# Six blocks instead of three between a gate matrix and its weights, one-hots one step earlier, low parts off GpSimd, and another order at the end of an encoder layer

## The chip, the cores and the metric

The kernel runs on one core of one Trainium2 chip. The metric is the device time of one execution in microseconds (us); the version before is the median of three runs. The core's engines are TensorE (PE in the rows: matmuls; PEld: its weight loads), VectorE (DVE), ScalarE (ACT), GpSimd (POOL) and SyncE (SP, which here only issues DMAs). Each engine works through its own instructions in order.

## The reference

One encoder layer for 512 tokens of width 2048, all in float32:

```
h = RMSNorm(x);  [q | k | v | x_gate | x_rec] = h @ W_in
A = windowed attention(q, k, v)              # 16 heads, 128-query blocks, a sink per head
B = gelu(x_gate) * (RG-LRU forward + RG-LRU backward)(conv(x_rec))
x = x + concat(RMSNorm(A), RMSNorm(B)) @ W_out
x = x + PEER(RMSNorm(x))                     # below
return RMSNorm(x)

PEER: q = xt @ W_pq -> 8 heads x 2 halves; top 16 of 128 keys in each half, top 16 of the sums:
      128 experts (of 16384) for each token, with softmax gates
      act = gelu(x . u_emb[e]);  out = sum over e of gate * act * v_emb[e]
```

## The kernel before

**Matmuls in three parts.** Every float32 operand is split into a high part `hi` (a cast on ScalarE, line 269) and a low part `lo = raw - hi` (a subtraction, line 281), and a product is three matmuls: hi by hi, hi by lo, lo by hi (`mm3`, lines 296 to 299). The weights come in units of 128 by 2048 (1 MB): `load` issues the DMA on SP into one of two `raw` buffers, `split` casts `hi` into one of two buffers and lists the low part, `flush_lo` makes the listed low parts, `take` splits up to the unit after the one that it hands out. So a unit's hi cast can start when the unit two before it has been multiplied. In the first stages `split` makes the low part at once; from the projection W_pq on (`st["defer"]`) it is made where `flush_lo` is called. `on_pool` (line 241) names nine units whose low part is made on GpSimd: seven that belong to W_out, split during the attention, and the first two of W_pq.

**Attention** (lines 704 to 834) is a generator with three steps for each of 32 pairs of heads and query blocks: scores (TensorE `ps_s`, VectorE mask, maximum and the small additions of lines 719 to 721), exponentials (ScalarE) with the transposes of an earlier pair, and the product with V (`ps_o`, VectorE `y_att`, line 757). Two more steps after each eight pairs transpose the output (`att_yt`). One step follows each of the 16 `mm3` of a W_out unit, so that the attention runs beside W_out's matmuls. `ps_s` and `ps_o` share two PSUM banks.

**The experts, in two ways.** 160 of the tokens (128 and `NB1` = 32) are done by gathering rows of u_emb and v_emb with indirect DMAs on GpSimd and multiplying on VectorE; `gather_gen` does one such step (some 2.3 us of VectorE) whenever it is called, a "tick". The other 352 tokens (`TD`) are done densely: 128 U blocks compute act for all experts (`u_block`: 16 times `mm3`, 48 matmuls, then a gelu into `ga`), and 16 groups of 8 V units multiply the weighted activations by v_emb (`v_unit`, also 48 matmuls each). In between, `weigh` multiplies `ga` by the gate matrix `G` (VectorE, line 1321) and splits the result into `Wh` (ScalarE, line 1324) and `Wl` (VectorE, line 1325). U blocks run ahead of their weighing; an activation that must wait long is spilled to DRAM (`ad`) and read back (`reload`, on SP, into three buffers `gr`).

**The gate matrix** is built in 88 steps of `NB` = 4 tokens beside the U blocks. `g_onehots` compares two lists of indices with an iota (one-hots `ohA` and `ohB`, two VectorE operations) and scales `ohA` by the gates, with one VectorE multiplication for even steps and four ScalarE operations for odd ones. `g_step` n first copies the result of step n-2 out of PSUM (`flush_evac`, ScalarE, line 1219, four banks `psA`), makes the one-hots of step n+3 (`G_AHEAD`), and multiplies ohB by ohA into `ps_G`. After each eight steps ScalarE issues a 2 MB DMA into `gd` in DRAM. `load_g` reads G back for four blocks at a time, on SP, once `gd` is written.

**The order** is fixed by `stage_plan` before anything runs: it keeps a clock for TensorE, VectorE and ScalarE, and puts tasks (routing, softmax, gate steps, ticks) into hooks, four per U block, each with costs in us. The first `lead0` = 40 U blocks come before any V unit: 37 with hooks, and three more, beside which the first nine blocks are weighed:

```
    load_g(0)
    load_g(1)
    for _ in range(3):
        reload()
    for i in range(3):
        u_block(lead0 - 3 + i, beside=lambda: beside(range((0, 3, 6)[i], (3, 6, PR + LEAD)[i])))
```

Then 8 V units and a run of U blocks alternate: six runs of three U blocks, one of seven, and eight or seven from there. `beside` makes, in this order, a tick if one is due, the low part, the additions of the V unit before (`v_evict`), the weighings, and further ticks. 55 activations are spilled.

**The end.** The last group has no U blocks. `final(q)` transposes a quarter of the accumulated output for three groups of tokens (twelve transposes into PSUM tiles `pt_f` of two pools with two banks each), adds the residual (VectorE, line 1451), and `out_piece` squares it on ScalarE into a tile `jk` of one of these pools and multiplies it by the final gain on GpSimd. Quarters 0 to 2 follow V units 5, 6 and 7; quarter 3 follows the last `v_evict`.

Of the kernel before, what the change touches and what calls it, by code (L numbers as in the profile page):

```python
# [8 lines left out]
F32 = mybir.dt.float32  # L9
# [32 lines left out]
LEAD = 1  # L42
NB = 4
G_AHEAD = 3
G_STEPS = [(tt, t) for tt in range(1, NT) for t in range(NB1 if tt == 1 else 0, 128, NB)]

C_GMIX = 0
# [10 lines left out]
def stage_plan():  # L58

    tasks = []
    for r in range(6):
        tasks += [("pair", 6.9, 0.0, 0.0)]
        if r < 4:
            tasks += [("tr", 0.0, 0.6, 0.6), ("sc", 6.8, 0.6, 1.3)]  # L70
        if r < 5:
            tasks += [("pick", 0.0, 2.5, 0.0)]
        tasks += {2: [("soft_a", 0, 0.9), ("soft_b", 0, 1.5), ("prime", 0.0, 0.0, 0.0)],
                  3: [("soft_a", 1, 0.9), ("soft_b", 1, 1.5)],
                  4: [("rep", 0.8, 0.0, 0.7)],
                  5: [("soft_a", 2, 1.7), ("free", 0.0, 0.0, 0.0), ("lists", 1), ("soft_b", 2, 1.7),
                      ("lists", 2)]}.get(r, [])
    tasks += [("pre", m) for m in range(G_AHEAD)]
    for n in range(len(G_STEPS)):
        if G_STEPS[min(n + G_AHEAD + 2, len(G_STEPS) - 1)] == (3, 0):  # L80
            tasks += [("lists", 3)]
        tasks += [("g", n)]
    hooks, ticks_on, since = [], False, 0.0
    pe, dve, act = 0.0, 4.0, 0.0
    while tasks:
        if len(hooks) % 4 == 0:
            dve, act = dve + 2.35, act + 2.4
        pe += 1.94
        cur = []
        while tasks and max(dve, act) <= pe:  # L90
            if ticks_on and since >= 3.5:
                cur.append(("tick", None))
                dve, since = dve + 2.35, 0.0
                continue
            t = tasks.pop(0)
            if t[0] == "g":
                cost, arg = ((1.37, 2.2, 1.22), (2.06, 0.6, 1.22))[t[1] % 2], t[1]
            elif t[0] == "pre":
                cost, arg = ((2.06, 0.0, 0.0), (1.37, 1.6, 0.0))[t[1] % 2], t[1]
            elif t[0] == "lists":  # L100
                cost, arg = (0.0, 0.5, 0.9), t[1]
            elif t[0] in ("soft_a", "soft_b"):
                cost, arg = (t[2], 0.5, 0.0), t[1]
            else:
                cost, arg = t[1:], None
            cur.append((t[0], arg))
            dve, act, pe = dve + cost[0], act + cost[1], pe + cost[2]
            if t[0] == "prime":
                ticks_on, since = True, -9.0
            if ticks_on:  # L110
                since += cost[0]
            if t[0] in ("tr", "soft_a", "lists"):
                break
        dve, act = max(dve, pe - 2), max(act, pe - 2)
        hooks.append(cur)
    nbg = -(-len(hooks) // 4)
    hooks += [[] for _ in range(4 * nbg - len(hooks))]
    lead0 = nbg + 3
    done, runs, order = lead0, [], [("u", b) for b in range(lead0)]
    order += [("w", b) for b in range(PR + LEAD)]  # L120
    for g in range(NP - 1):
        b0 = (g + 1) * PR
        r = NBLK - done if g == NP - 2 else min(max(3, b0 + PR + LEAD - done), NBLK - done)
        todo, run = list(range(b0 + LEAD, b0 + PR)), []
        if g:
            order.append(("w", b0))
        for i in range(r):
            ready = [b for b in todo if b < done + i]
            now = ready[:-(-len(todo) // (r - i))]
            todo = todo[len(now):]  # L130
            run.append(now)
            order += [("w", b) for b in now] + [("u", done + i)]
        assert not todo or todo == [NBLK - 1]
        order += [("w", b) for b in todo]
        done += r
        runs.append(run)
    seen, spilled = [], set()
    for kind, b in order:
        if kind == "u":
            seen.append(b)  # L140
        elif b < seen[-1] - 1:
            spilled.add(b)
    return hooks, lead0, runs, spilled
# [3 lines left out]
def tile_encoder(  # L147
# [90 lines left out]
    N3 = 18  # L238
    U_P3 = 16 + 12
    U_P5 = U_P3 + 16  # L240
    on_pool = set(range(U_P3 + 2, U_P3 + 9)) | {U_P5, U_P5 + 1}
    on_both = set()
    st = {"next": 0, "split": 0, "xp": None, "defer": False}
    parts = {}
# [954 lines left out]

    As, Bs, evac, gst = {}, {}, [], {}  # L1200

    def g_onehots(n):
        tm, ta = G_STEPS[n]
        lt = lts[tm]
        Bs[n] = B = gst["oh"].tile([128, NB, 128], F32, tag="B", name="ohB", bufs=G_AHEAD + 1)
        As[n] = Ao = gst["oh"].tile([128, NB, 128], F32, tag="A", name="ohA", bufs=G_AHEAD + 1)
        for o, j in ((Ao, 0), (B, 1)):
            V.tensor_tensor(o, io_sb.unsqueeze(1).to_broadcast([128, NB, 128]),
                            lt[:, j, ta:ta + NB].unsqueeze(2).to_broadcast([128, NB, 128]), op=ALU.is_equal)
        if n % 2:  # L1210
            for t in range(NB):
                A.activation(out=Ao[:, t, :], in_=Ao[:, t, :], func=AF.Copy, scale=lt[:, 2, ta + t:ta + t + 1])
        else:
            V.tensor_tensor(Ao, Ao, lt[:, 2, ta:ta + NB].unsqueeze(2).to_broadcast([128, NB, 128]), op=ALU.mult)

    def flush_evac(keep=1):
        while len(evac) > keep:
# [4 lines left out]

    def g_step(n):
        flush_evac()
        if n + G_AHEAD < len(G_STEPS):
            g_onehots(n + G_AHEAD)
        tt, ta = G_STEPS[n]
        B, Ao = Bs.pop(n), As.pop(n)
        at, o = divmod((tt - 1) * 128 + ta - NB1, TB)
        if o == 0:  # L1230
            gst["stg"] = gst["p"].tile([128, NBLK, TB], F32, tag="stg", name="stg")
        ps = psA.tile([128, NB, 128], F32, tag="A", name="ps_G")
        for t in range(NB):
            T.matmul(ps[:, t, :], B[:, t, :], Ao[:, t, :], start=True, stop=True)  # L1234
        evac.append((gst["stg"], o, ps, gd[:, at] if o + NB == TB else None))
# [44 lines left out]

    flush_lo()
    psS[:] = [psA, "A"]
    for b in range(lead0 - 3):
        hk = iter(hooks[4 * b:4 * b + 4])

        def hook():
            for name, arg in next(hk):
                do[name](arg)

        u_block(b, hook)  # L1290
# [38 lines left out]
        if b in ad_at:  # L1329
            reload()  # L1330

    due = {"now": 0.0, "per": (2 * (NSLOT + NB1) - ticks["n"]) / (2 * NBLK - PR - lead0 + 3)}

    late_ev = []

# [13 lines left out]
            due["now"] -= 1.0  # L1349
            next(gg, None)  # L1350

    load_g(0)
    load_g(1)
    for _ in range(3):
        reload()
    for i in range(3):
        u_block(lead0 - 3 + i, beside=lambda: beside(range((0, 3, 6)[i], (3, 6, PR + LEAD)[i])))

    def v_unit(g, c, ws, gather=True):
        hi, lo = take()  # L1360
# [23 lines left out]
    def final_gen():  # L1384
# [21 lines left out]
        for o, i, r0, n in ((o1, 1, 128, NB1), (x2[0], 0, 0, 128)):  # L1406
            for c in range(4):
                d = slice(c * 512, (c + 1) * 512)
                jk = psB.tile([128, 512], F32, tag="B", name="jk")
                A.activation(out=jk[0:n], in_=o[0:n, d], func=AF.Square, accum_out=gf_t["sq"][0:n, i, c:c + 1])  # L1410
            r = out_rstd(i, n)
            yield
            V.scalar_tensor_tensor(out=o[0:n], in0=o[0:n], scalar=r[0:n], in1=gf[0:n], op0=ALU.mult, op1=ALU.mult)
            nc.sync.dma_start(out=out[r0:r0 + n, :], in_=o[0:n])
            if i == 1:
                gf_t["o"].append(gat.tile([128, D], F32, tag="gat", name="o"))
            yield

    def out_rstd(i, n):
        sq = stat.tile([128, 1], F32, tag="sqx", name="sqo")  # L1420
# [7 lines left out]

    def out_piece(i, c, o, n):
        d = slice(c * 512, (c + 1) * 512)  # L1430
        jk = psB.tile([128, 512], F32, tag="B", name="jk")
        A.activation(out=jk[0:n], in_=o[0:n, d], func=AF.Square, accum_out=gf_t["sq"][0:n, i, c:c + 1])
        P.tensor_tensor(o[0:n, d], o[0:n, d], gf_t["gf"][0:n, d], op=ALU.mult)

# [20 lines left out]
    for g in range(NP):  # L1455
        b0 = (g + 1) * PR
        for c in range(8):
            pss = v_unit(g, c, (b0,) if c == 1 and 0 < g < NP - 1 else (), g < NP - 1)
            late_ev.append((g, c, pss))
            if g == NP - 1:  # L1460
                next(fin, None)
                if c in (5, 6, 7):
                    final(c - 5)
        if g == NP - 1:
            break
        for ws in runs[g]:
            u_block(ub, beside=lambda: beside(ws))
            ub += 1
        if g == NP - 2:
            weigh(NBLK - 1)  # L1470
        if g == NP - 2:
            for _ in gg:
                pass
            fin = final_gen()
            next(fin)
# [81 lines left out]
```

## Time and profile before

| what | value |
|---|---|
| median of 3 runs | 3059.82 us (3058.1 to 3060.89) |
| the profiled execution | 3060.12 us |
| its span, first to last instruction | 3058.3 us, mean granted clock 0.986 |
| busy: TensorE, VectorE, ScalarE, GpSimd | 96%, 74%, 38%, 28% of the span |
| data moved | 766.76 MB, mean 251 GB/s |

The span is what the profile resolves; the time of the execution is 1.8 us longer. A busy share is a mean over stages with different limits, so the rows below are read by stage.

### The profile page before, as it was taken

What the parts mean: (1) busy time and instruction counts of PE and PEld (TensorE: products, weight loads), DVE (VectorE), ACT (ScalarE), POOL (GpSimd) and SP (SyncE); (2) the same over time, 40 slices, a digit from 0 to 9 for tenths busy, and PEclk for the clock granted to TensorE, in tenths of its full rate; (3) what the DMA queues carried; (4) which work ended last, traced back from release to release, by engine and by line L of the source; (5) the groups of instructions that cost most, each with busy time, mean ns of one, the idle gap of its engine ahead of it and who ended that gap; (6) DMA issues with size and microseconds to landing.
All of it is one profiled execution on the core that took longest, in us unless ns stands there. A gap on an engine that the chain in (4) does not pass through costs nothing. (4 is left out here: it accounts for less than half of the span.)

```text
span 3058.3 us, 41550 instructions
## 1 busy us (share of the span) xinstructions
PE 2933.6 (96%) x16965; PEld 2729.7 (89%) x16965; DVE 2272.5 (74%) x3143; ACT 1153.3 (38%) x1529; POOL 846.3 (28%) x539
## 2 busy tenths in 40 slices
PE   8999989999999989979999999999999999999997
PEld 6777867788889988979999999999999999999996
DVE  5773367444987789857888888888787887888874
ACT  5663244343444455523322232323323233232233
POOL 0000121022545113423323433233232333233312
PEclk9999999999999999989999999999999999999998
DMA  5222220133225777789899998988889898898983
GB/s 228 76 85 87 85 109 29 69 131 121 83 101 194 258 281 291 298 316 338 335 337 358 355 345 332 343 335 336 328 333 338 326 342 339 340 343 322 349 300 114
DMA packets 160623, 766.76 MB, mean 251 GB/s; under 512 B 13744, under 2 KB 72896, under 8 KB 74480
## 3 DMA queue, kind: packets, MB, share of 16 engines
q1 hardware_dynamic: 101712, 378.44, 33.8%
q0 software_dynamic: 48000, 345.73, 29.9%
q10 hardware_dynamic: 10720, 39.93, 3.4%
q8 instruction: 133, 2.18, 0.3%
q14 instruction: 58, 0.48, 0.0%
HBM read 722.42 MB, written 41.63 MB: 250 GB/s over the span
## 5 line engine op out<-in xcount | busy, mean ns | idle before, releaser
L281 DVE TENSOR_TENSOR lo<-raw,hi 128x2048 fp32r<-128x2048 f32 x307 | 708.5, 2308 | 456.2 <-ACT hi L269 454.0
L269 ACT CAST hi<-raw 128x2048 fp32r<-128x2048 f32 x316 | 602.4, 1907 | 764.5 <-PE ps_v L1369 517.1
L297 PE MATMUL ps_u<-H,hi 128*128 128x352 f32 x2048 | 666.8, 326 | 14.9 <-ACT hi L269 14.9
L299 PE MATMUL ps_u<-H,lo 128*128 128x352 f32 x2048 | 662.5, 323 | 14.3 <-DVE lo L281 14.3
L1368 PE MATMUL ps_v<-Wh,hi 128*128 128x352 f32 x2048 | 664.0, 324 | 6.8 <-ACT Wh L1324 6.2
L1370 PE MATMUL ps_v<-Wh,lo 128*128 128x352 f32 x2048 | 663.6, 324 | 7.2 <-DVE lo L281 7.2
L1369 PE MATMUL ps_v<-Wl,hi 128*128 128x352 f32 x2048 | 663.4, 324 | 0.8
L298 PE MATMUL ps_u<-L,hi 128*128 128x352 f32 x2048 | 661.3, 323 | 0.0
L1147 POOL DMA_INDIRECT gu<-in_u_emb_dram,idx x160 | 331.6, 2073 | 691.4 <-DVE x L1173 500.9
L1147 POOL DMA_INDIRECT gv<-in_v_emb_dram,idx x160 | 286.7, 1792 | 658.8 <-DVE gu L1154 466.1
L299 PEld LDWEIGHTS ps_u<-H,lo 128*128 128x128 f32 x2048 | 385.6, 188 | 17.7 <-DVE lo L281 17.7
L297 PEld LDWEIGHTS ps_u<-H,hi 128*128 128x128 f32 x2048 | 385.9, 188 | 15.4 <-ACT hi L269 15.2
L1368 PEld LDWEIGHTS ps_v<-Wh,hi 128*128 128x128 f32 x2048 | 386.7, 189 | 10.8 <-ACT Wh L1324 8.0
L1370 PEld LDWEIGHTS ps_v<-Wh,lo 128*128 128x128 f32 x2048 | 386.4, 189 | 8.3 <-DVE lo L281 8.3
L1369 PEld LDWEIGHTS ps_v<-Wl,hi 128*128 128x128 f32 x2048 | 386.5, 189 | 2.2 <-DVE Wl L1325 2.2
L298 PEld LDWEIGHTS ps_u<-L,hi 128*128 128x128 f32 x2048 | 385.9, 188 | 0.0
L1154 DVE SCALAR_TENSOR_TENSOR gu<-gu,xng 128x2048 f32<-128x2048 f32 x160 | 364.8, 2283 | 4.2 <-DMA gu<-in_u_emb_dram,idx 4.2
L1173 DVE SCALAR_TENSOR_TENSOR x<-gv,w,x 128x2048 f32<-128x2048 f32 x128 | 300.1, 2345 | 2.9 <-DMA gv<-in_v_emb_dram,idx 2.6
L1123 ACT ACTIVATE ga<-ps_u 128x352 f32<-128x352 f32 x128 | 59.1, 462 | 195.3 <-PE ps_u L299 194.3
L1324 ACT CAST Wh<-ga 128x352 fp32r<-128x352 f32 x73 | 35.5, 487 | 223.3 <-DVE ga L1321 223.3
L297 PE MATMUL ps_cm<-xh,hi 128*128 128x512 f32 x256 | 106.0, 414 | 11.5 <-ACT xh L369 9.1
L1234 PE MATMUL ps_G<-ohA,ohB 128*128 128x128 f32 x704 | 92.0, 279 | 25.4 <-ACT stg L1219 17.4
(311 smaller groups left out, 3792.3 us busy)
## 6 DMA issues: line engine op xcount, KB each, us to landing
raw<-in_u_t_dram SPq DMA_DIRECT2D x128, 1024.0 KB, 6.2
raw<-in_v_t_dram SPq DMA_DIRECT2D x128, 1024.0 KB, 9.0
raw<-in_w_dram SPq DMA_DIRECT2D x28, 1024.0 KB, 4.8
gd<-stg ACTq DMA_DIRECT2D x11, 2048.0 KB, 10.1
G<-gd SPq DMA_DIRECT2D x32, 704.0 KB, 11.0
raw<-in_w_out_dram SPq DMA_DIRECT2D x16, 1024.0 KB, 4.7
raw<-in_w_pq_dram SPq DMA_DIRECT2D x16, 1024.0 KB, 5.0
ad<-ga ACTq DMA_DIRECT2D x55, 176.0 KB, 3.5
```

The source lines that it names most:

```text
L269: A.copy(hi, raw)
L281: en.tensor_tensor(lo[:, c], raw[:, c], hi.bitcast(F32)[:, c], op=ALU.subtract)
L297: T.matmul(ps, ah, bh, start=first, stop=False)
L298: T.matmul(ps, ah, bl, start=False, stop=False)
L299: T.matmul(ps, al, bh, start=False, stop=last)
L1147: P.indirect_dma_start(out=g, out_offset=None, in_=u_emb if kind == "u" else v_emb, in_offset=bass.IndirectOffsetOnAxis(ap=ix, axis=0))
L1154: V.scalar_tensor_tensor(out=g, in0=g, scalar=1.0, in1=xs_t["x"], op0=ALU.mult, op1=ALU.mult, accum_out=a_t[h][:, k:k + 1])
L1173: V.scalar_tensor_tensor(out=d, in0=g, scalar=wk, in1=d, op0=ALU.mult, op1=ALU.add)
L1234: T.matmul(ps[:, t, :], B[:, t, :], Ao[:, t, :], start=True, stop=True)
L1368: T.matmul(ps[:, 0:TD], hi[:, cc], Wh, start=j == 0, stop=False)
L1369: T.matmul(ps[:, 0:TD], hi[:, cc], Wl, start=False, stop=False)
L1370: T.matmul(ps[:, 0:TD], lo[:, cc], Wh, start=False, stop=j == PR - 1)
```

## The change

Five edits. (1) `N_TRANS` = 6: six U blocks, not three, stand between the last hooked block and the first V unit. The first three weigh nothing; the three re-reads follow the first of them and the two reads of G the second; the weighings stand beside the last three. (2) `g_onehots` makes ohA one step earlier than ohB; an even step's multiplication follows its ohA at once, an odd step's scaling on ScalarE is emitted with its ohB. ohA has five buffers and ohB four. (3) The planner ends a hook after an odd gate step, and plans four first one-hot tasks at equal cost instead of three. Worked through with its new numbers it gives 38 hooked blocks (before: 37), `lead0` = 44 (40), 34 ticks in the hooks (33), 61 spilled activations (55), and seven runs of three U blocks (six, and one of seven). (4) `on_pool` is empty: all low parts are made on VectorE. (5) In the last group, `final` of quarters 0 to 2 comes before V units 5 to 7 and not after them, and the squares are written to an SBUF tile (`jk_tile`, of the pool that held G).

```diff
+N_TRANS = 6
...
-    tasks += [("pre", m) for m in range(G_AHEAD)]
+    tasks += [("pre", m) for m in range(G_AHEAD + 1)]
...
-                cost, arg = ((2.06, 0.0, 0.0), (1.37, 1.6, 0.0))[t[1] % 2], t[1]
+                cost, arg = (1.8, 0.6, 0.0), t[1]
...
-            if t[0] in ("tr", "soft_a", "lists"):
+            if t[0] in ("tr", "soft_a", "lists") or t[0] == "g" and t[1] % 2:
                 break
...
-    lead0 = nbg + 3
+    lead0 = nbg + N_TRANS
...
-    on_pool = set(range(U_P3 + 2, U_P3 + 9)) | {U_P5, U_P5 + 1}
+    on_pool = set()
...
+    def g_one(lt, ta, j):
+        o = gst["oh"].tile([128, NB, 128], F32, tag="AB"[j], name="oh" + "AB"[j], bufs=G_AHEAD + 2 - j)
+        V.tensor_tensor(o, io_sb.unsqueeze(1).to_broadcast([128, NB, 128]),
+                        lt[:, j, ta:ta + NB].unsqueeze(2).to_broadcast([128, NB, 128]), op=ALU.is_equal)
+        return o
...
+        if n < len(G_STEPS):
+            tm, ta = G_STEPS[n]
+            As[n] = g_one(lts[tm], ta, 0)
+            if n % 2 == 0:
+                V.tensor_tensor(As[n], As[n], lts[tm][:, 2, ta:ta + NB].unsqueeze(2).to_broadcast([128, NB, 128]),
+                                op=ALU.mult)
+        n -= 1
+        if 0 <= n < len(G_STEPS):
+            tm, ta = G_STEPS[n]
+            Bs[n] = g_one(lts[tm], ta, 1)
+            if n % 2:
+                for t in range(NB):
+                    A.activation(out=As[n][:, t, :], in_=As[n][:, t, :], func=AF.Copy,
+                                 scale=lts[tm][:, 2, ta + t:ta + t + 1])
...
-        if n + G_AHEAD < len(G_STEPS):
-            g_onehots(n + G_AHEAD)
+        g_onehots(n + G_AHEAD + 1)
...
-    load_g(0)
-    load_g(1)
-    for _ in range(3):
-        reload()
-    for i in range(3):
-        u_block(lead0 - 3 + i, beside=lambda: beside(range((0, 3, 6)[i], (3, 6, PR + LEAD)[i])))
+    for i in range(N_TRANS):
+        ws = ((), (), (), range(3), range(3, 6), range(6, PR + LEAD))[i]
+        u_block(lead0 - N_TRANS + i, beside=lambda: beside(ws))
+        if i == 0:
+            for _ in range(3):
+                reload()
+        if i == 1:
+            load_g(0)
+            load_g(1)
...
-        jk = psB.tile([128, 512], F32, tag="B", name="jk")
+        jk = jk_tile()
...
+    def jk_tile():
+        t = gp.tile([128, NTB, GRP, TB], F32, tag="G", name="jk")
+        return t.rearrange("p a g t -> p (a g t)")[:, 0:512]
...
         for c in range(8):
+            if g == NP - 1 and c > 4:
+                final(c - 5)
             pss = v_unit(g, c, (b0,) if c == 1 and 0 < g < NP - 1 else (), g < NP - 1)
             late_ev.append((g, c, pss))
             if g == NP - 1:
                 next(fin, None)
-                if c in (5, 6, 7):
-                    final(c - 5)
```

## Rows read from the trace of the kernel before

**Rows 1.** The page: busy time by engine, and the costliest groups (busy, mean ns).

```profile
PE 2933.6 (96%) x16965; PEld 2729.7 (89%) x16965; DVE 2272.5 (74%) x3143; ACT 1153.3 (38%) x1529; POOL 846.3 (28%) x539
...
L281 DVE TENSOR_TENSOR lo<-raw,hi 128x2048 fp32r<-128x2048 f32 x307 | 708.5, 2308 | 456.2 <-ACT hi L269 454.0
```

**Rows 2.** Windows: busy time (instructions) of each engine, clock, DMA share, GB/s.

```profile
400.00:600.00 200.00, 185.74 (x990) 140.31 (x987) 127.98 (x307) 90.67 (x245) 27.78 (x7) 0.94 0.12 44
1000.00:1300.00 300.00, 274.56 (x1888) 268.36 (x1887) 262.06 (x306) 158.41 (x319) 83.93 (x32) 1.00 0.75 281
1309.00:1360.00 51.00, 31.12 (x160) 29.78 (x160) 31.07 (x31) 15.36 (x19) 13.93 (x6) 0.77 0.86 302
1370.00:1400.00 30.00, 30.00 (x187) 30.00 (x186) 19.18 (x13) 10.56 (x13) 9.15 (x6) 1.00 0.91 345
1400.00:1800.00 400.00, 386.27 (x2364) 381.59 (x2363) 326.63 (x294) 119.07 (x107) 131.71 (x67) 0.99 0.92 344
```

**Rows 3.** Timeline of ScalarE, SP, VectorE and TensorE, 1293 to 1324 us.

```profile
1293.75 0.47 ACT L1123 ACTIVATE ga<-ps_u 128x352 f32<-128x352 f32 x1 [2.20 <-PE ps_u L299]
...
1295.72 0.33 ACTq L1221 DMA_DIRECT2D gd<-stg  x1
...
1308.99 1.49 SPq L1315 DMA_DIRECT2D G<-gd  x2
...
1317.21 0.53 DVE L1321 TENSOR_TENSOR gr<-gr,G 128x352 f32<-128x352 f32 x1 [16.89 <-DMA gr<-ad]
...
1322.04 1.90 ACT L269 CAST hi<-raw 128x2048 fp32r<-128x2048 f32 x1 [0.40 <-ACT ga L1123]
...
1323.99 0.66 PE L297 MATMUL ps_u<-H,hi 128*128 128x352 f32 x1 [14.92 <-ACT hi L269]
```

**Rows 4.** Groups of instructions by line, 1000 to 1300 us.

```profile
L1234 PE MATMUL ps_G<-ohA,ohB 128*128 128x128 f32 x704 | 92.0, 279 | 25.4 <-ACT stg L1219 17.4 <-DVE ohB L1208 4.7 <-DVE ohA L1214 2.0
...
L1208 DVE TENSOR_TENSOR ohA<-io_sb,lt 128x512 f32<-128x512 f32 x88 | 60.0, 682 | 0.0
...
L1212 ACT ACTIVATE ohA<-ohA,lt 128x128 f32<-128x128 f32 x176 | 56.4, 391 | 112.2 <-DVE ohA L1208 112.2
```

**Rows 5.** Timeline of ScalarE and TensorE, 1127 to 1136 us.

```profile
1127.62 1.28 ACT L1212 ACTIVATE ohA<-ohA,lt 128x128 f32<-128x128 f32 x4 [2.99 <-DVE ohA L1208]
...
1135.64 1.16 PE L1234 MATMUL ps_G<-ohA,ohB 128*128 128x128 f32 x8 [2.73 <-ACT stg L1219]
```

**Rows 6.** Timeline of GpSimd, VectorE, ScalarE and TensorE, 410 to 448 us.

```profile
410.24 4.53 POOL L281 TENSOR_TENSOR lo<-raw,hi 128x2048 fp32r<-128x2048 f32 x1 [15.07 <-ACT hi L269]
...
410.80 3.99 DVE L719 TENSOR_TENSOR m_att<-m_att,sink_sb 128x2 f32<-128x2 f32 x1
...
415.90 0.70 PE L711 MATMUL ps_s<-kT,qT 64*128 64x256 f32 x2 [2.19 <-DVE y_att L757]
...
438.97 0.29 DVE L757 TENSOR_TENSOR y_att<-ps_o,den 128x128 f32<-128x128 f32 x1 [0.23 <-PE ps_o L751]
...
439.73 1.89 ACT L269 CAST hi<-raw 128x2048 fp32r<-128x2048 f32 x1
...
447.62 0.86 PE L740 MATMUL pt_att<-id_sb,s_att 128*128 128x128 f32 x3 [3.60 <-DVE yt L772]
```

**Rows 7.** Timeline of ScalarE and VectorE, 683 to 691 us.

```profile
683.51 1.89 ACT L269 CAST hi<-raw 128x2048 fp32r<-128x2048 f32 x1
...
685.91 4.87 DVE L893 TENSOR_TENSOR L<-pt_x,H 128x512 fp32r<-128x512 f32 x8 [2.17 <-ACT H L892]
```

**Rows 8.** Waits of TensorE over the whole span: total, times, longest.

```profile
PE ps_s L711 <- DVE y_att L757: 10.1, 5, 2.3
...
PE pt_f L1449 <- ACT jk L1432: 4.6, 4, 1.2
```

**Rows 9.** Timeline of TensorE and VectorE after the last V unit.

```profile
3036.78 1.04 PE L1449 MATMUL pt_f<-id_sb,acc 128*96 128x128 f32 x8
...
3040.27 0.94 DVE L1380 TENSOR_TENSOR acc<-ps_v,acc 128x352 f32<-128x352 f32 x2
```

More of the change, by code (lines that the diff above doesn't have):

```diff
@@ L1200, in tile_encoder @@
     As, Bs, evac, gst = {}, {}, [], {}
-    def g_onehots(n):
[L1203 to L1214, printed above, removed]
+    def g_one(lt, ta, j):
[3 more added lines that the diff above has]
+        return o
+    def g_onehots(n):
+        if n < len(G_STEPS):
[12 more added lines that the diff above has]
+                                 scale=lts[tm][:, 2, ta + t:ta + t + 1])
     def flush_evac(keep=1):
@@ L1282, in tile_encoder @@
     psS[:] = [psA, "A"]
-    for b in range(lead0 - 3):
+    for b in range(lead0 - N_TRANS):
         hk = iter(hooks[4 * b:4 * b + 4])
@@ L1330, in weigh @@
             reload()
-    due = {"now": 0.0, "per": (2 * (NSLOT + NB1) - ticks["n"]) / (2 * NBLK - PR - lead0 + 3)}
+    due = {"now": 0.0, "per": (2 * (NSLOT + NB1) - ticks["n"]) / (2 * NBLK - PR - lead0 + N_TRANS)}
     late_ev = []
@@ L1430, in out_piece @@
         d = slice(c * 512, (c + 1) * 512)
-        jk = psB.tile([128, 512], F32, tag="B", name="jk")
+        jk = jk_tile()
         A.activation(out=jk[0:n], in_=o[0:n, d], func=AF.Square, accum_out=gf_t["sq"][0:n, i, c:c + 1])
```

## The prediction

> **What bounds the kernel now.** I read the page first [rows 1]. TensorE is busy for 2933.6 of 3058.3 us, so whatever the change does, it can only give back what lies in the other 124.7 us and in slow-clock time; every other engine has room over the whole span. The question is therefore where TensorE stands still, and the windows answer it [rows 2]. The steady part needs nothing: at 1370 to 1400 us TensorE is busy throughout, with 187 matmuls in 30 us, that is 0.160 us each and 7.7 us for a block of 48. Three stages fall short of that: the attention (400 to 600 us, 14.3 us idle, mean clock 0.94), the building of the gate matrix (1000 to 1300 us, 25.4 us idle at full clock) and the passage from the gate matrix to the weights (1309 to 1360 us, 19.9 us idle, clock 0.77). A fourth, thinner loss lies in 1400 to 1800 us: 13.7 us idle, in the groups of three U blocks between eight V units.
>
> Then I followed each stage by its order in time. **The passage** [rows 3]: the last hooked block ends with its gelu at 1293.75; call that T0. ScalarE issues the last write of the gate matrix at T0+2.0, the read of G leaves SP only when that write has landed, at T0+15.2, and VectorE's first weigh, which needs G and the re-read activations queued behind it, starts at T0+23.5. The weighing is emitted beside the first block after T0. ScalarE is in order, so the cast of the hi part for the third block stands behind three Wh casts and that block's gelu, and comes at T0+28.3. TensorE has two blocks of work (15.4 us), then waits 14.9 us.
>
> **The gate matrix** [rows 4]: the ps_G matmuls wait 25.4 us, 17.4 of them for ScalarE's copies of ps_G, which free the four banks. ScalarE itself stands 112.2 us waiting for VectorE's one-hots, on 44 occasions, in front of those copies. One case in time [rows 5]: ScalarE waits 2.99 us for a one-hot until 1127.62, the block ends meanwhile, its hi cast comes before the next copy, and TensorE waits 2.73 us for that copy, until 1135.64. The cause is three gate steps in one hook: step n takes the bank of n-4, whose copy is emitted in step n-2, here only in the same hook.
>
> **Attention** [rows 6]: while GpSimd makes a low part (410.24 to 414.77), a VectorE addition of 128 by 2 elements, both inputs in SBUF, takes 3.99 us; TensorE then waits 2.19 us for what VectorE does after it. The seven low parts of this stage all do so; six of these waits are 13.7 us, 10.1 [rows 8] and the 3.6 us at 447.62. Behind the attention [rows 7] two more are made while VectorE works from PSUM. **The end** [rows 8, 9]: the transposes of the output wait four times, 4.6 us in all, for the ScalarE squares, which share their PSUM banks, and those of the third quarter come after the last V unit, so that its accumulation runs on VectorE only at 3040.27, 3.5 us after the last V matmul.
>
> **The change, part by part.**
>
> *Six blocks.* A block is only moved, so no matmul is added. Now three blocks run after T0 without weighing, and the fourth starts at T0+23.1, when G is due (T0+23.5 before, and G no longer shares its turn with three re-reads: these now leave SP one block earlier). On SP, the loads of blocks that stand behind the G read need a buffer that is freed only at about T0+19, later than T0+15.2, so holding SP delays none of them. If G lands late, the next to suffer is the hi cast for the sixth block, emitted behind the three weighings and needed at T0+38.5; with weighing done by about T0+30 there are some 6 us of slack. What is recovered: 51 us with 160 matmuls, at 187 in 30 us, are 25.7 us of work, so 25.3 us are lost now (19.9 idle, the rest slow clock behind the stall). Some of it stays, since a V unit behind a fresh weighing waits a little: 2.5 us, as in the groups of 1400 to 1800 us. **Gain 23**, bounds 12 (G 10 us later) and 25.
>
> *Its price.* Working the planner's loop with the new numbers gives 38 hooked blocks instead of 37, 44 leading blocks instead of 40, 61 spilled blocks instead of 55, and seven groups of three U blocks instead of six (the seventh had seven). 13.7 us idle in 400 us is 3 us for a group of 11 units: **loss 3**, bounds 0 and 6. Six more writes and re-reads of 176 KB are six small DMAs beside a TensorE that is not waiting for them: nothing, and if that cover fails, it is part of the 6.
>
> *One-hots and pairs.* The same instructions are made: per gate step two comparisons of 0.68 us on VectorE, and either a multiplication there or four scalings on ScalarE. What moves is that a scaling reads a one-hot compared one step earlier, so most of ScalarE's 112.2 us of waiting goes; and the planner ends a hook after an odd step, so that the plan has no hook with three steps. The copy that a step needs was then emitted in the hook before, a quarter block earlier. I take the 17.4 us of copies as gone but for 3, and the 3.1 us for ohA (25.4 less 17.4 and 4.7, with rounding) as gone; the 4.7 us for ohB stay, since B is made no earlier. **Gain 17.5**. Room on VectorE is the limit: 262.1 us of 300 now; one more block adds a low part and about one gather step, 2.3 us each, so 267 in a stage of 300+7.7-17.5 = 290 us, 92%. It fits, but with little to spare: bounds 4 (only the scaling's own waits go) and 23.
>
> *Low parts on VectorE.* A low part costs VectorE 2.31 us [rows 1] instead of GpSimd 4.53. But it stands in VectorE's order behind a ScalarE cast of 1.9 us. Where in the attention's steps it falls decides. Counting 16 steps per unit, three of the seven (the second, fourth and sixth) come right after the scores: VectorE arrives about 0.5 us behind the addition that is held now, the hi part is ready, and VectorE is free again some 1.2 to 1.5 us earlier than now: gains of 1.5, 1.0 and 1.5. Two (the fifth, seventh) come after y_att: now the next scores wait, which moves the stall forward, -0.4 and +0.5. The first: -0.25. The third comes between scores and y_att: the hi cast begins at 439.73 [rows 6], so VectorE, which before comes to y_att at 438.97 and is done with it at 439.3, stands until the cast is done at 441.6 and with the low part until 443.9; y_att follows at 444.7, TensorE waits 5.4 us there and not 3.6 us later: -1.9. Sum +2; another 2 where a stall short enough no longer lowers the clock. Against that the two behind the attention [rows 7]: the hi cast ends at 685.4, the low part then holds VectorE to 687.7 and the L parts, now from 685.91, start 1.8 us later; with the first of the two delaying the same chain by 1.8 us before it, TensorE loses about 4. **Net 0**. Bounds: a gain of 14 (the 13.7 us of stalls gone, nothing in their place) and a loss of 13: a stall of 5.4 us with its slow clock is 9.9 (the stage has 14.3 us idle and, at 0.94 over 200 us, 12 us of slow clock, so 1.84 us for each us of stall); four of the nine like that make 39.6, less the 26.3 us that the stage loses now.
>
> The Trainium skill (SBUF — State Buffer, Who interferes with whom) says that a VectorE instruction with two SBUF inputs and a GpSimd instruction that reads SBUF exclude each other for the whole instruction. The 3.99 us addition agrees. By that rule alone the stalls go with the GpSimd instructions and the sum would be some 14 us lower; it doesn't speak of the wait for the hi cast.
>
> *The end.* The squares go to an SBUF tile, so two waits of 1.15 us before the last unit go, and the twelve transposes of the third quarter (1.6 us, at 1.04 for eight) come before it: it ends 0.7 us earlier. Its accumulation then starts at once, 3.3 us earlier, and the last quarter loses its wait of 1.15 us: **gain 5**, bounds 2 and 7. The hi cast for unit 6 now stands behind three squares, some 4 us after unit 4 ends; with cast and low part (1.9 and 2.3) that is 8.5 us at most, and unit 6 starts 1.6 + 7.7 + 1.6 = 10.9 us after unit 4 ends. No cost; with that cover gone, a us or two.
>
> **Sum.** 23 + 17.5 + 5 - 3 + 0 = 42.5 us. The profiled execution took 3060.1 us (span 3058.3), 0.3 above the median of 3059.8; I forecast 3060.1 - 42.5 = **3017.6 us**.
>
> **Rivals.**
> *VectorE becomes the bound of the gate matrix.* For: 87% busy there now, 92% then. Against: TensorE's waits are for ScalarE's copies rather than for B. Gain 4 instead of 17.5: 3031 us.
> *G is late again.* For: write, read and re-reads are a chain of 21.5 us in a stage where the DMA queues are near full. Against: the slack above. Gain 12 instead of 23: 3029 us.
> *The GpSimd stalls go and nothing replaces them*, 14 more: 3004 us. For: VectorE is busy only 128 of 200 us there [rows 2]. Against: the place of the third low part.
> *The other side: low parts in VectorE's order hold the attention.* Each could cost what the third costs before its relief, 9.9 us with its slow clock: nine make 89, less the 26 us lost there now, a loss of 63, and the time is 3017.6 + 63 = 3081 us. It decides from (42.5 + 26)/9 = 7.6 us each. Against: three of nine have their hi part ready.
>
> **Chances.** Forecast 0.60; VectorE bound 0.14; late G 0.09; stalls gone 0.13; held attention 0.04. The first four, 0.96, are all faster by more than 0.2% (6 us, about what a measurement of this kernel tells from no change); of these I leave 0.02 to several bad bounds at once, which end near no change. The last is slower. So faster 0.94, same 0.02, slower 0.04. The range 2999 to 3042 takes in the three faster rivals with some of their own spread and leaves out the last and combinations of the bad bounds.
>
> **What would show it.** Passage: no TensorE wait over 3 us between the last gate step and the first V unit, clock near 1 there, first weigh at about T0+24 or later. Gate matrix: ScalarE's wait for ohA under 40 us, ps_G's wait for copies under 4, VectorE above 90%. Attention: the 128 by 2 additions well under 1 us, lo on VectorE with a wait for the hi cast in front, TensorE idle about as now; around 685 us a TensorE wait of 1 to 3 us that is not there now. End: no wait for squares, accumulation right behind the last matmul. The forecast is wrong if ps_G waits turn to ohB, if the first weigh still holds a hi cast, or if waits of TensorE behind VectorE's low parts exceed 30 us before 700 us.

## The result, and the profile after

The changed kernel took 3021.48 us (median of four runs, 3015.97 to 3025.28) beside 3058.96 us for the kernel before on the same chip: ratio 0.9878, 95% interval 0.9858 to 0.9899. A second set, with the experiments, gave 3018.42 beside 3059.79: 0.986 (0.9839 to 0.9881). It is faster by 37 to 41 us; 42.5 were forecast. The profiled execution is the fastest of its set (3015.97 us), so the stages below add up to more than the medians.

The page of the changed kernel, beside [rows 1]; 316 low parts are on VectorE now, none on GpSimd:

```profile
span 3014.2 us, 41581 instructions
PE 2922.0 (97%) x16965; PEld 2723.4 (90%) x16965; DVE 2272.7 (75%) x3152; ACT 1152.2 (38%) x1529; POOL 771.9 (26%) x530
L282 DVE TENSOR_TENSOR lo<-raw,hi 128x2048 fp32r<-128x2048 f32 x316 | 731.2, 2315 | 460.1 <-ACT hi L270 458.9
```

The kernels are best compared between TensorE's own marks (first and last matmul into a PSUM tile), with the work that moved from stage to stage taken out at 0.160 us for a matmul:

| stretch | before, us | after, us | matmuls | net, us |
|---|---|---|---|---|
| start to first ps_l | 373.0 | 370.3 | same | -2.7 |
| attention beside W_out, first to last ps_l | 212.3 | 200.9 | same | -11.4 |
| to the last ps_p of W_pq | 293.0 | 298.4 | same | +5.4 |
| U with the gate matrix, to the last ps_G | 413.2 | 404.8 | +36 | -14.2 |
| passage, to the first ps_v | 44.7 | 58.9 | +156 | -10.8 |
| V units, to the last ps_v | 1700.4 | 1664.1 | -180 | -7.4 |
| to the end of the span | 21.7 | 16.8 | -12 | -3.0 |

The nets sum to the 44.1 us by which the spans differ. The 12 matmuls of the last row are the transposes of the third quarter, which now come before the last V unit. The first row is not the change's doing: in other runs of kernels with the same code there it lies between 370 and 373 us. One trace of each kernel carries chance in the other rows too. In the experiments' traces of kernels with the same code in a stage, the attention takes 212.3 to 216.7 us before the change and 197.3 to 202.3 after it, at the same idle time (16.1 and 10.2 or 10.3 us) and another mean clock; the passage takes 43.5 to 45.7 and 52.6 to 59.3 us, the V units after the change 1663.4 to 1669.9. A net of a few us in one of these rows is therefore not a measurement by itself.

Windows of the changed kernel, beside [rows 2] (columns as there: PE, PEld, DVE, ACT and POOL, then the clock, the DMA share and GB/s): the attention, the start of W_pq, the gate matrix twice, the passage, and the first V units.

```profile
400.00:571.00 171.00, 163.02 (x914) 121.08 (x914) 111.19 (x298) 83.78 (x236) 0.00 (x0) 0.96 0.10 38
665.00:685.00 20.00, 16.20 (x78) 13.06 (x77) 12.23 (x18) 10.43 (x17) 5.89 (x4) 0.91 0.60 235
1000.00:1279.00 279.00, 266.00 (x1855) 262.66 (x1854) 261.55 (x304) 154.78 (x317) 42.95 (x30) 1.00 0.79 295
1050.00:1250.00 200.00, 188.94 (x1329) 186.48 (x1328) 194.40 (x230) 114.76 (x240) 33.29 (x23) 1.00 0.84 316
1274.40:1333.30 58.90, 54.20 (x315) 53.04 (x314) 39.67 (x32) 18.73 (x22) 12.24 (x8) 0.94 0.95 354
1400.00:1800.00 400.00, 393.88 (x2436) 391.62 (x2435) 337.51 (x306) 121.83 (x110) 145.38 (x70) 1.00 0.94 356
```

In the passage TensorE is idle for 4.7 us at clock 0.94, where 51 us had 19.9 idle at 0.77. But the DMA engines are 0.95 busy there (0.86 before), and VectorE is busy 194.4 of 200 us in the middle of the gate matrix.

Groups of the gate matrix, 1000 to 1279 us, beside [rows 4]:

```profile
L1243 PE MATMUL ps_G<-ohA,ohB 128*128 128x128 f32 x704 | 90.5, 276 | 13.0 <-DVE ohB L1205 11.3 <-ACT stg L1229 1.7
...
L1223 ACT ACTIVATE ohA<-ohA,lt 128x128 f32<-128x128 f32 x176 | 56.4, 392 | 94.3 <-DVE ohA L1205 94.3
```

The wait for copies fell from 17.4 to 1.7 us, but that for ohB rose from 4.7 to 11.3, and ScalarE still waits 94.3 us for one-hots.

Timeline of the passage, beside [rows 3]; the gelu that the prediction calls T0 starts at 1278.57 here:

```profile
1278.57 0.47 ACT L1124 ACTIVATE ga<-ps_u 128x352 f32<-128x352 f32 x1 [3.45 <-PE ps_u L300]
...
1280.55 0.33 ACTq L1231 DMA_DIRECT2D gd<-stg  x1
...
1291.87 12.96 SPq L1324 DMA_DIRECT2D G<-gd  x2
...
1295.96 1.91 ACT L270 CAST hi<-raw 128x2048 fp32r<-128x2048 f32 x1 [1.56 <-DMA raw<-in_u_t_dram]
...
1307.49 1.90 ACT L270 CAST hi<-raw 128x2048 fp32r<-128x2048 f32 x1 [5.41 <-DMA raw<-in_u_t_dram]
...
1311.77 0.43 PE L300 MATMUL ps_u<-H,lo 128*128 128x352 f32 x1 [1.74 <-DVE lo L282]
1312.33 0.52 DVE L1330 TENSOR_TENSOR gr<-gr,G 128x352 f32<-128x352 f32 x1 [0.61 <-DMA G<-gd]
...
1320.04 1.90 ACT L270 CAST hi<-raw 128x2048 fp32r<-128x2048 f32 x1 [3.28 <-DMA raw<-in_u_t_dram]
```

The first weighing waits only 0.61 us for G. But it starts at T0+33.8, when G has landed, and not at T0+24: G is some 10 us later than forecast, and that costs little only because the block beside which the weighing stands is late itself. What holds TensorE now is the raw U data: three hi casts wait for it, 10.3 us in all, and the low parts and TensorE follow them.

Timeline of the attention around the third low part, beside [rows 6], and of the start of W_pq, beside [rows 7]:

```profile
427.75 0.16 DVE L720 TENSOR_TENSOR m_att<-m_att,sink_sb 128x2 f32<-128x2 f32 x1
...
435.94 2.29 DVE L282 TENSOR_TENSOR lo<-raw,hi 128x2048 fp32r<-128x2048 f32 x1 [3.17 <-ACT hi L270]
...
438.96 0.47 PE L771 MATMUL pt_y<-id_sb,y_att 128*128 128x128 f32 x1 [3.52 <-DVE y_att L758]
...
673.37 2.80 DVE L282 TENSOR_TENSOR lo<-raw,hi 128x2048 fp32r<-128x2048 f32 x1 [1.70 <-ACT hi L270]
...
676.83 3.42 PE L886 MATMUL pt_x<-id_sb,xn 128*128 128x128 f32 x16 [2.47 <-DVE L L894]
```

The 128 by 2 addition takes 0.16 us instead of 3.99. VectorE stands 3.17 us for the hi cast, and TensorE behind it 3.52 us.

The end, beside [rows 9]: the last quarter's transposes wait 0.29 us, and no wait for squares is left.

```profile
2997.72 0.53 DVE L1392 TENSOR_TENSOR acc<-ps_v,acc 128x352 f32<-128x352 f32 x1 [3.35 <-PE ps_v L1382]
2998.30 1.19 PE L1465 MATMUL pt_f<-id_sb,acc 128*96 128x128 f32 x9 [0.29 <-DVE acc L1392]
```

### The profile page after: what moved, and what is told of

Its sections match the earlier page's. It is cut to its first block, busy times and chain, and to the rows that moved or that the text cites. A ratio compares the mean times of both kernels' runs of the same rounds, so it can differ in the third digit from the quotient of the medians.

```text
span 3014.2 us, 41581 instructions
## 1 busy us (share of the span) xinstructions
PE 2922.0 (97%) x16965; PEld 2723.4 (90%) x16965; DVE 2272.7 (75%) x3152; ACT 1152.2 (38%) x1529; POOL 771.9 (26%) x530
## 5 line engine op out<-in xcount | busy, mean ns | idle before, releaser
L282 DVE TENSOR_TENSOR lo<-raw,hi 128x2048 fp32r<-128x2048 f32 x316 | 731.2, 2315 | 460.1 <-ACT hi L270 458.9
L1148 POOL DMA_INDIRECT gv<-in_v_emb_dram,idx x160 | 298.7, 1867 | 655.2 <-DVE gu L1155 460.4
L1148 POOL DMA_INDIRECT gu<-in_u_emb_dram,idx x160 | 286.3, 1789 | 696.5 <-DVE x L1174 501.4
L1392 DVE TENSOR_TENSOR acc<-ps_v,acc 128x352 f32<-128x352 f32 x240 | 114.0, 517 | 5.4 <-PE ps_v L1382 5.3
L298 PE MATMUL ps_cm<-xh,hi 128*128 128x512 f32 x256 | 105.4, 412 | 11.4 <-ACT xh L370 9.1
```

What stands on the lines that cost most here:

```text
L282: en.tensor_tensor(lo[:, c], raw[:, c], hi.bitcast(F32)[:, c], op=ALU.subtract)
L298: T.matmul(ps, ah, bh, start=first, stop=False)
L1148: P.indirect_dma_start(out=g, out_offset=None, in_=u_emb if kind == "u" else v_emb, in_offset=bass.IndirectOffsetOnAxis(ap=ix, axis=0))
L1392: V.tensor_tensor(d, ps[:, 0:TD], d, op=ALU.add)
```

## Experiments

**Four parts, each alone in the kernel before.** (The front shows the diff; each kernel has only the named edits. All four shared one chip, where the kernel before took 3062.54 us.)

*Six blocks.*

```diff
-    lead0 = nbg + 3
+    lead0 = nbg + N_TRANS
...
+        ws = ((), (), (), range(3), range(3, 6), range(6, PR + LEAD))[i]
```

> The kernel before with the six blocks alone. Theory (parts add up; read off the two traces): the passage gains about 16 us with the extra group of three already in it, so about 3043 us against 3059. My forecast had 23 - 3 = 20 for it: 3039. Rival (the passage is bound by the DMA engines, not by where the weighing stands): less than 8 us gained, TensorE still waiting over 10 us in all between the last gate step and the first V unit.

Measured 3045.35 us, ratio 0.9942 (0.9929 to 0.9956): 17.2 us faster. Four hi casts of its passage wait for raw data (0.94, 3.40, 4.00 and 2.29 us) with the DMA engines fully busy.

*One-hots and pairs.*

```diff
-            if t[0] in ("tr", "soft_a", "lists"):
+            if t[0] in ("tr", "soft_a", "lists") or t[0] == "g" and t[1] % 2:
...
-            g_onehots(n + G_AHEAD)
+        g_onehots(n + G_AHEAD + 1)
```

> The kernel before with the one-hots and the planner's pairs alone; three blocks in the passage as before. Theory: about 14 us gained (forecast 17.5), the waits of ps_G for ScalarE's copies under 4 us and those for ohB 8 to 12 us. Rival (VectorE is the bound of that stage): gain of 4 us or less, ohB waits above 18 us.

Measured 3050.64 us, 0.9955 (0.9941 to 0.9968): 11.9 us faster. The waits are already those of the full change: ohB 11.3, copies 1.7 us, VectorE 194.4 of 200 us busy.

```profile
1050.00:1250.00 200.00, 189.29 (x1332) 186.38 (x1331) 194.43 (x231) 115.70 (x243) 34.89 (x23) 1.00 0.82 306
```

So they come from this edit alone, not from the low parts on VectorE. Its two halves, the earlier ohA and the planner's pairs, were not run apart.

*Low parts on VectorE.*

```diff
-    on_pool = set(range(U_P3 + 2, U_P3 + 9)) | {U_P5, U_P5 + 1}
+    on_pool = set()
```

> The kernel before with all low parts on VectorE and nothing else. Theory: the stage of W_out with the attention becomes about 11 us shorter and that of W_pq about 5 us longer, 6 us gained in all: 3053. My forecast had 0 for it (4 gained, 4 lost). Rival (the lock alone): 14 us gained, no loss at W_pq. Rival (holding): slower by 10 us or more.

Measured 3055.6 us, 0.9976 (0.9965 to 0.9986): 6.9 us faster. The attention takes 200.6 us, W_pq ends 298.4 us after it, as in the full change.

*The end.*

```diff
-                jk = psB.tile([128, 512], F32, tag="B", name="jk")
+                jk = jk_tile()
...
+            if g == NP - 1 and c > 4:
+                final(c - 5)
...
-                if c in (5, 6, 7):
-                    final(c - 5)
```

> The kernel before with the order of the last group and the SBUF tile for the squares alone. Theory: 5 us gained, nearly all behind the last V matmul (21.7 us from there to the end of the span before, about 17 expected). Rival (the moved transposes delay the low part of the next unit): 2 us or less, with new waits of TensorE for lo in the last three units.

Measured 3059.26 us, 0.9986 (0.9977 to 0.9996): 3.3 us faster; the last V matmul lies 16.7 us before the end of the span (21.7 before). The four parts sum to 39.3 us: they hardly meet.

**Four variants of the changed kernel** (kernel before on their chip: 3062.67 us).

*W_pq's low parts back on GpSimd.* These are the first two alone, the two that GpSimd made before; "every other one" in the expectation is a slip.

```diff
-    on_pool = set()
+    on_pool = {U_P5, U_P5 + 1}
```

> The changed kernel with the low parts of W_pq alone (every other one of them, as before the change) on GpSimd again; the attention's stay on VectorE. Theory: the 5.4 us that the stage of W_pq and the routing lost (199.5 us before, 204.9 after) come from VectorE making all its low parts; the stage returns to 199 to 201 us and the time against the kernel before falls from 0.9878 to about 0.986 (-5 us). Rival: the loss comes from what W_pq's stage inherits from the attention (VectorE's backlog at its start); then the stage stays at 203 to 205 us and the ratio at 0.9878.

Measured 3013.7 us, 0.984 (0.9826 to 0.9853). W_pq ends 293.0 us after the attention, as before the change. Its window, beside the same 20 us above:

```profile
665.00:685.00 20.00, 19.77 (x100) 15.77 (x99) 10.77 (x16) 11.27 (x15) 10.51 (x5) 1.00 0.67 263
```

So the two low parts on VectorE cost 5.4 us, in waits and in clock (1.00 against 0.91).

*No gathers beside the first three passage blocks.*

```diff
-    due = {"now": 0.0, "per": (2 * (NSLOT + NB1) - ticks["n"]) / (2 * NBLK - PR - lead0 + N_TRANS)}
+    due = {"now": 0.0, "per": (2 * (NSLOT + NB1) - ticks["n"]) / (2 * NBLK - PR - lead0 + N_TRANS - 3)}
...
-        u_block(lead0 - N_TRANS + i, beside=lambda: beside(ws))
+        u_block(lead0 - N_TRANS + i, beside=lambda: beside(ws, i > 2))
```

The first line spreads the gathers that are left out over all units that follow.

> The changed kernel with no gathers of embedding rows beside the first three of the six passage blocks, so that the 16 DMA engines have less to move there (they are 0.97 to 1.15 busy from 1280 to 1325 us in the changed kernel). Theory A, the DMA engines are full: G's issue ends in well under the 6.5 us that each of its two took, the raw loads of the fourth to sixth block come in time, and TensorE's waits in the passage fall from 7.7 us to under 4; the time is 2 to 5 us shorter (ratio 0.9862 to 0.9872), unless the gathers cost it later. Theory B, the order on SP's queue alone (the loads stand behind G's issue whatever the engines do): waits in the passage stay at 7 to 8 us and the ratio at 0.9878 or above.

Measured 3020.64 us, 0.9864 (0.9849 to 0.9879). SP's queue and ScalarE in the passage, then its window:

```profile
1294.12 3.95 SPq L1324 DMA_DIRECT2D G<-gd  x2
...
1294.92 1.91 ACT L270 CAST hi<-raw 128x2048 fp32r<-128x2048 f32 x1 [0.52 <-DMA raw<-in_u_t_dram]
...
1274.40:1324.50 50.10, 50.10 (x316) 50.10 (x315) 29.95 (x25) 18.55 (x22) 6.35 (x4) 1.00 0.88 313
```

The issue of G takes 3.95 us and not 12.96, one cast waits 0.52 us for raw data, and TensorE never stops from the last gate step to the first V unit: 58.9 us become 50.1. By the windows, some 5 MB less are moved there (313 GB/s over 50.1 us against 354 over 58.9). The total is no shorter than the changed kernel's (0.9864 beside 0.986 and 0.9878), since the V units give it back: they take 1675.6 us, against 1663.4 to 1669.9 in the kernels with the gathers in place, and the two longest waits there (3.45 and 4.55 us, at 1530 and 1622 us) are again behind hi casts that wait for raw data, one of them:

```profile
1617.17 1.90 ACT L270 CAST hi<-raw 128x2048 fp32r<-128x2048 f32 x1 [6.45 <-DMA raw<-in_v_t_dram]
```

The gathers that were left out of the passage are made there, where the DMA engines were 0.94 busy without them. That they cause these waits is not shown: from 1400 to 1800 us the share in this run is 0.93, no higher.

*G a block later.*

```diff
-        if i == 1:
+        if i == 2:
             load_g(0)
```

> The changed kernel with the load of G issued one block later (behind the third of the six blocks). Theory A, the DMA engines are full: raw loads and G share the same bandwidth, so the raw loads come earlier and G later by a block; TensorE's waits in the passage change place (the last block's wait for G grows from 2.98 us to 5 or more) and the sum stays at 6 to 9 us; ratio 0.987 to 0.989. Theory B, the order on SP's queue: the raw loads no longer stand behind G's issue, G still comes in time with a block to spare, and the waits fall to under 4 us; ratio 0.986 to 0.987.

Measured 3023.56 us, 0.9882 (0.9867 to 0.9897). G now leaves SP in 1.71 us, but the loads issued ahead of it are still late, and G is too:

```profile
1295.36 1.90 ACT L270 CAST hi<-raw 128x2048 fp32r<-128x2048 f32 x1 [3.55 <-DMA raw<-in_u_t_dram]
...
1299.99 1.71 SPq L1324 DMA_DIRECT2D G<-gd  x2
...
1304.38 1.90 ACT L270 CAST hi<-raw 128x2048 fp32r<-128x2048 f32 x1 [4.89 <-DMA raw<-in_u_t_dram]
...
1312.79 0.53 DVE L1330 TENSOR_TENSOR gr<-gr,G 128x352 f32<-128x352 f32 x1 [4.19 <-DMA G<-gd]
```

TensorE's waits, up to and in the first V unit, sum to 10.1 us instead of 7.7; 6 to 9 were expected if the DMA engines are full, under 4 if the order counts. So the order on SP's queue is not the cause. With the run before, that leaves what the DMA engines have to move in these 50 us.

*All scaling on ScalarE.*

```diff
-            if n % 2 == 0:
-                V.tensor_tensor(As[n], As[n], lts[tm][:, 2, ta:ta + NB]...
...
-            if n % 2:
-                for t in range(NB):
+            for t in range(NB):
```

> The changed kernel with every one-hot's scaling on ScalarE (four activations of 392 ns), where the changed kernel does every other one by a VectorE multiplication of 692 ns; VectorE is 97% busy from 1050 to 1250 us there and ScalarE 57%. Theory, VectorE is the bound of the gate matrix: without some 35 multiplications (24 us of the 200) it is 85 to 88% busy, TensorE's waits for ohB fall from 11.3 us to under 3, and the time is 6 to 10 us shorter (ratio 0.9845 to 0.986). Rival, the way from one-hot to matmul is too short and ScalarE's hi casts come first: then waits for ohA and for the copies of ps_G take the place of those for ohB, and the ratio stays at 0.987 to 0.989.

Measured 3019.42 us, 0.9859 (0.9844 to 0.9874), and 404.3 us for the stage instead of 404.8: nothing. VectorE is busy 171.2 of 200 us, yet waits for ohB are 8.2 us and for copies 3.6. Its window, one stretch of its VectorE timeline, and the TensorE wait that follows:

```profile
1050.00:1250.00 200.00, 188.69 (x1324) 185.83 (x1323) 171.23 (x195) 153.88 (x380) 36.38 (x23) 1.00 0.84 313
...
1241.68 2.29 DVE L282 TENSOR_TENSOR lo<-raw,hi 128x2048 fp32r<-128x2048 f32 x1 [3.14 <-ACT hi L270]
1243.89 2.34 DVE L1174 SCALAR_TENSOR_TENSOR x<-gv,w,x 128x2048 f32<-128x2048 f32 x1
1246.16 0.68 DVE L1205 TENSOR_TENSOR ohA<-io_sb,lt 128x512 f32<-128x512 f32 x1
...
1247.59 1.13 PE L1239 MATMUL ps_G<-ohA,ohB 128*128 128x128 f32 x8 [2.66 <-DVE ohB L1205]
```

A wait for the hi cast (3.14), the low part (2.29) and a gather piece (2.34) in a row leave 7.6 us without a one-hot, from 1238.55 to 1246.16: more than the look-ahead holds. Three of the four waits for ohB come behind such gaps of over 7 us. In the changed kernel itself, with VectorE 97% busy, the longest gap from 1000 to 1280 us is 5.9 us: its three longest waits for ohB (1.7, 1.7 and 2.3 us) stand behind gaps of 5 to 6 us, the others behind shorter ones.

**A second pair and their sum, beside the changed kernel itself** (kernel before: 3059.79 us).

> The changed kernel itself once more, beside the three below on one chip, so that they are compared with it directly. Its ratio to the kernel before should fall again in 0.986 to 0.990.

Measured 3018.42 us, as told above.

*W_out's low parts three attention steps later.*

```diff
     ag = att_gen()
+    st["defer"] = True
...
                     next(ag, None)
+                    if kk == 0 and tt == 2:
+                        flush_lo()
...
+    st["defer"] = False
```

> The changed kernel with the low part of each W_out block issued three steps of the attention later, so that VectorE does not stand still for ScalarE's hi cast (11.1 us in five waits from 370 to 571 us of the changed kernel). Theory, what TensorE still waits for in the attention (3.8 + 3.5 + 1.5 us and two small ones) comes from VectorE held by that wait: its wait for hi falls under 3 us, TensorE's waits from about 10 us to about 5, and the stage from 200.9 to 194 to 198 us, since the clock gains too (ratio 0.9855 to 0.987). Rival, they come from VectorE's own 2.29 us for each low part: the waits change place and the stage stays at 200 to 202 us.

Measured 3012.13 us, 0.9838 (0.9821 to 0.9856). The stage takes 192.9 us instead of 200.9. VectorE's waits for the hi cast in the attention, in the changed kernel and here, and the stage's window:

```profile
DVE lo L282 <- ACT hi L270: 11.1, 5, 3.2
...
DVE lo L282 <- ACT hi L270: 1.7, 2, 1.4
...
371.00:564.00 193.00, 186.11 (x1046) 139.47 (x1044) 131.84 (x341) 99.71 (x268) 8.60 (x12) 0.98 0.18 66
```

VectorE waited 11.1 us for the cast, now 1.7; the stage gains somewhat more than expected. Some of the 8 us can be the clock's chance: the stage without this edit took 197.3 us in one trace, at equal idle time. TensorE's idle time in the stage fell from 10.3 to 6.9 us.

*U's low parts a quarter of a block later, with all scaling on ScalarE.*

```diff
             if hook and k % 4 == 3:
-                flush_lo()
+                if k > 3:
+                    flush_lo()
                 hook()
```

> Every one-hot scaled by ScalarE, as in the run above where that alone left TensorE's waits for ohB at 8.2 us (VectorE 86% busy, but 56.7 us of waiting for hi casts between 870 and 1276 us), and in addition the low part of each U block issued a quarter of a block later, so that VectorE does not wait for the hi cast. Theory, order on VectorE: a wait for hi, the low part of 2.29 us and one or two gather pieces of 2.3 us in a row leave 6 us without a one-hot, more than the look-ahead of three steps; without the wait TensorE's waits for ohB fall under 4 us and the stage from the end of W_pq to the last matmul of G from 404.3 to 398 to 401 us. Rival, VectorE's work by itself: the waits for ohB stay at 7 to 11 us and the stage at 404 us.

Measured 3004.76 us, 0.981 (0.979 to 0.9829). The stage takes 392.5 us (404.3 with the scaling alone). TensorE's waits for ohB and VectorE's for the cast, 870 to 1275 us, and the window:

```profile
PE ps_G L1240 <- DVE ohB L1206: 0.5, 1, 0.5
...
DVE lo L282 <- ACT hi L270: 50.4, 27, 7.2
...
1050.00:1250.00 200.00, 197.98 (x1404) 196.86 (x1403) 182.13 (x206) 163.18 (x404) 40.38 (x25) 1.00 0.88 331
```

The waits for ohB are gone, but not as the theory had it: VectorE still waits 50.4 us for the cast (56.7 with the scaling alone). What went are the long rows: between 1030 and 1270 us the gaps of over 7 us without a one-hot, counted along VectorE's timeline, fell from four to one, since some of the wait now lies behind a gather piece. How much the later low parts would give with the old scaling was not run.

*All three edits.*

> The three edits together: the first two low parts of W_pq on GpSimd, the low parts of W_out issued later, and ScalarE's scaling with the later low parts of U. If each is worth what its own run showed and they don't meet, the gains against the changed kernel add up: 5 us for W_pq, 3 to 6 for the attention, 3 to 6 for the gate matrix; 3005 to 3012 us, ratio 0.981 to 0.984. If VectorE's time is what is left everywhere, the later two give nothing and the ratio is that of the first alone, 0.984 to 0.986.

Measured 2991.59 us, 0.9767 (0.9749 to 0.9785), 26.8 us below the changed kernel on the same chip and better than expected. The single gains add up: by its trace 5 us for W_pq, 6 for the attention, 13 for the gate matrix. Its passage still takes 56.8 us.

## Why the prediction was right, point by point

**Six blocks and their price: 20 forecast, 17 to 18 measured.** Alone they gave 17.2; in the full change passage and V units net 18.2. The weighings hold no hi cast, and TensorE's longest wait up to the first V unit is 1.74 us (2.98 in it), as stated; the clock there is 0.94 and not near 1. G's date was wrong by 10 us: the weighing was to be done by about T0+30 and ended at T0+38. So the rival "G is late again" was right in its cause and not in its price, since the blocks themselves came late. The step that failed is the one on the raw loads, "holding SP delays none of them": they were late, and 8.5 us stay lost in the passage (58.9 us less 315 matmuls of 0.160). The holding is the lesser part of it: only one of the three late loads stood behind G on SP, the other two had left before it, at 1285.17 and 1291.43 us. What its sum put at nothing is that transfers on the way slow each other. Leaving out gathers restored the passage in full and moving G did not, so G, raw blocks and gathered rows together want more than the DMA engines move. How much that costs varies: with the same blocks and gathers the passage took 52.6 us in the run with U's later low parts. As the V units then lost about as much, nothing was won by moving the gathers there. The price of 3 us didn't show: TensorE's idle time from 1400 to 1800 us fell from 13.7 to 6.1, and over all V units from 19.9 to 17.0. Why was not tested.

**One-hots and pairs: 17.5 forecast, 12 alone and 14 by the stage.** The copies went as stated (1.7 us, under 4), and VectorE is above 90%, as stated. Two statements were wrong: the waits for ohB did not stay at 4.7 us but rose to 11.3, and ScalarE's wait for ohA is 94.3 us, not under 40. The first is a sign that the prediction itself named for being wrong: with 11.3 of 13.0 us the waits of ps_G did turn to ohB. The second says that its reason was wrong: the copies came in time although ScalarE waits nearly as long for one-hots as before, which speaks for the planner's pairs and not for the earlier ohA (not run apart). The rival that VectorE becomes the bound is half right. With the scaling on ScalarE, the bound is not VectorE's busy share, since 23 us less of work in 200 changed nothing, but its order: rows of low part and gather piece with a wait for the cast in front outlast the look-ahead; shortened, with VectorE at 182 of 200 us, TensorE loses 2 us of these 200 in place of 11. Whether order or work holds the changed kernel itself, where no such row is over 5.9 us, is not shown, since the later low parts were not run with its scaling.

**Low parts on VectorE: 0 forecast, 6 to 7 measured.** This was the largest mis-sizing. The place of the worst stall was right (y_att of the third low part), its size 3.5 us instead of 5.4. The stage's idle waits fell by some 6 us (16.1 to 10.3) where 2 were forecast, and the clock gave more than the 2 forecast: a mean of 0.944 over 212 us is some 12 us of slow clock, 0.966 over 200.9 some 7. W_pq lost 5.4 where 4 were forecast, at the place named (2.47 and 1.14 us of waits, at 670 to 677 us, as the chain runs some 10 us earlier here); giving its two back to GpSimd regained them. The Trainium skill (SBUF — State Buffer, Who interferes with whom) speaks of the exclusion between the two engines; the 0.16 us addition, with GpSimd idle in the attention, agrees. The rival by that rule alone, 14 us more with nothing in the stalls' place, fell: waits for the hi cast did take part of it, and they went when the low parts came later.

**The end: 5 forecast, 3.3 alone and 3.0 by the stage,** with no wait for squares and the accumulation right behind the last matmul.

So the sum, 42.5, was met by terms that erred in both directions: 5 to 8 too much for gate matrix and passage, 6 to 7 too little for the low parts. That they cancelled to within 1 to 5 us is luck.

## What to carry to other kernels

When a stage is near the limit of two engines or of the DMA engines, a moved transfer is not free because its own chain has slack: count all the bytes of that stage first. Look-ahead can be used up by a long row of other work on the producing engine, whatever its busy share; look for a wait for another engine in that row before taking work off. Stalls cost their clock as well: size a stage's recovery from its mean clock, not from its idle time alone, and take more than one trace, since the clock of the same stage varies between them.

## What the runs showed of the hardware

The issue of a load on SP's queue can itself be held: the same two loads of G took 1.49 us in the kernel before [rows 3], 12.96 in the changed kernel, 3.95 without gathers beside them and 1.71 a block later. Full DMA engines alone do not set its length: their share while the loads are issued is 0.04 in the first case, and 1.02, 1.04 and 1.03 in the others.

```profile
1309.00:1310.50 1.50, 0.07 (x1) 0.00 (x0) 0.00 (x0) 0.00 (x0) 0.00 (x0) 1.00 0.04 12
1291.87:1304.83 12.96, 12.96 (x83) 12.96 (x82) 8.81 (x6) 2.84 (x3) 3.05 (x2) 1.00 1.02 414
1294.12:1298.07 3.95, 3.95 (x27) 3.95 (x26) 1.20 (x1) 2.19 (x2) 0.00 (x0) 1.00 1.04 405
1300.00:1301.70 1.70, 1.70 (x13) 1.70 (x12) 1.70 (x1) 0.00 (x0) 0.00 (x0) 1.00 1.03 433
```

What does was not tested; what is still under way on the same queue, in the changed kernel three re-reads and two raw loads, is the nearest candidate. The hold passes to whatever stands behind it on the queue: in the changed kernel the next raw load left SP only at 1304.91.
